# Weights of the output projections loaded piece by piece between the steps of other projections, each split one piece behind its DMA

## The chip, the cores and the metric

The kernel runs on one core of a Trainium2 chip. The metric is the device time of one execution in microseconds: the median of three runs, 1205.65 us before the change (1203.87 to 1205.76). The rows below come from one profiled execution of 1204.9 us, whose recorded span is 1203.1 us.

## The reference

A two-layer decoder trunk on x of 1024 tokens by 1024 columns, all in fp32 (P = 128 tokens make a block, so there are 8 blocks):

```
layer 0: h = rms_norm(x) * g;  z = h @ w_in
         z -> MLA q-latent, kv-latent, rope key | SWA q, k, v | gate
         MLA: 8 heads, causal attention          -> 512 columns
         SWA: 8 heads, window 128, ALiBi, sinks  -> 512 columns
         x1 = x + (concat(MLA, SWA) * silu(gate)) @ w_out      (1024x1024)
layer 1: h = rms_norm(x1) * g;  z = h @ w_in -> q, k, v, forget logits, gate
         16 heads, causal attention with cumulative log-forget bias
         x2 = x1 + (heads * silu(gate)) @ w_out                (1024x1024)
out = rms_norm(x2) * g_final
```

The change concerns the two products with `w_out`, the output projections.

## The kernel before, in words

Every fp32 product is made of three matmuls. An operand is split into a high part, the cast of the raw fp32 to fp32r, and a low part, raw minus high (`split_sb`, L109: the cast on ScalarE, L110, the subtraction on GpSimd or, if told so, VectorE, L111). `mm3` (L113) then adds high by high (L114), high by low and low by high (L115, L116). In the rows, `wh` and `wl` are the parts of an operand that lies in small tiles, `hh` and `hl` those of large ones: the normalised activations, and later the weights of the output projections. `kx` holds the weights of the windowed heads' output projection.

Every raw operand goes through the tag `wr`, which has four buffers (L74); `wh` and `wl` have three each. A DMA into `wr` can start when the split that reads that buffer's former content has ended. All these DMAs are issued by SyncE, in its own order.

Heads are the units of the main loop. A causal unit computes logits (`s`) row by row, the row's maximum (VectorE, L314), exponential (ScalarE, L321) and normalisation (GpSimd, L276), transposes the rows on PE (`t`, L347), splits them into `ph` (ScalarE, L102) and `pl` (VectorE, L103), and multiplies by v (`o`, L338 and L339). When a unit is done `o_evac` (L263) copies half of its output on ScalarE (`ob`, L267) and adds the rest on VectorE. Between these steps `Filler` runs steps of projections, one `mm3` at a time; strings of letters (`W_MLA_END` and so on) say where on PE each step stands, and PE's order is written by hand from them. The other engines' orders come from a scheduler that sees the program order and the buffers; an engine then takes its instructions in that fixed order.

`Filler` has two lists. `work` (projections) advances one step at a time; `loads` runs to its end at once as soon as its conditions are met. The output projections are these:

- `swa_wo(q)` (L888) loads four pieces of 128x512 of w_out's lower half for columns half q and splits each, in one go: for q = 0 as the load `wp`, for q = 1 in the last step of `p07` (L912). `swa_out(q, blk)` (L897), the work `p00` to `p07` and `p10` to `p17`, loads a 128x(4x128) operand of gated heads from `ogs0` (L901) and makes four steps.
- `load_wo` (L956) loads the other pieces: for layer 0 eight (four for each half of the columns) as the load `wo0` after `gate3`, the last gate projection; for layer 1 sixteen, eight of them when the first half of gate 6 is evacuated (`and_load`, L1140 on), the other eight two at a time in each `out1_first`. Its splits alternate between GpSimd and VectorE.
- `out0(nh, blk)` (L1018) and `out1_first(nh, blk)`, the work `first00` to `first13`, load their operand through `out_parts` (L971; DMA in L979) and make four steps each (`out_proj`, L986).

Of the kernel before, what the change touches and what calls it, by code (L numbers as in the profile page):

```python
# [18 lines left out]
P = 128  # L19
S = 1024  # L20
D = 1024
NB = S // P
# [37 lines left out]
def trunk(ctx, tc, x, positions, e_g_in, e_w_in, e_g_q_a, e_w_q_up, e_g_kv_a, e_w_kv_up,  # L60
# [45 lines left out]
            return nc.vector.scalar_tensor_tensor(out=lo, in0=src, scalar=gain, in1=hi.bitcast(F32),  # L106
                                                  op0=ALU.mult, op1=ALU.subtract).ins

    def split_sb(hi, lo, raw, engine=None):  # L109
        nc.scalar.copy(out=hi, in_=raw)  # L110
        (engine or nc.gpsimd).tensor_tensor(out=lo, in0=raw, in1=hi.bitcast(F32), op=ALU.subtract)  # L111

    def mm3(o, ah, al, bh, bl, first, last):  # L113
# [302 lines left out]
    class Filler:  # L416


        def __init__(self):
            self.work, self.loads, self.done = [], [], set()  # L420

        def add(self, name, gen, after=()):

# [2 lines left out]
        def load(self, name, gen, after=()):  # L426
            self.loads.append((name, gen, after))

        def free(self, items):
            return items and all(a in self.done for a in items[0][2])  # L430

        def ahead(self):

# [5 lines left out]

        def step(self):  # L440
            self.ahead()
            if self.free(self.work):
                try:
                    next(self.work[0][1])
                except StopIteration:
                    self.done.add(self.work.pop(0)[0])
                    self.step()

        def need(self, *names, ready=None):
            for name in names:  # L450
                while name not in self.done and not (ready and ready()):
                    self.ahead()
                    if name not in self.done:
                        assert self.free(self.work), (name, self.work[0], self.loads[:1])
                        self.step()

        def drain(self):
            while self.work or self.loads:
                self.ahead()
                assert self.free(self.work) or not self.work, self.work[0]  # L460
                self.step()

    fill = Filler()

# [421 lines left out]


    def swa_wo(q):  # L888
        tiles = [sbt("kx", [2, 512], F32R) for _ in range(4)]
        swa["wo"] = [(tiles[e // 2][:, e % 2, :], tiles[2 + e // 2][:, e % 2, :]) for e in range(4)]  # L890
        for e, (wh, wl) in enumerate(swa["wo"]):
            raw = sbt("wr", [512])
            for at, row in ((A, 512), (B, 768)):
                nc.sync.dma_start(out=raw[at], in_=wo0[row + 64 * e:row + 64 * e + 64, 512 * q:512 * (q + 1)])
            split_sb(wh, wl, raw)

    def swa_out(q, blk):  # L897
# [12 lines left out]
        nc.vector.tensor_tensor(out=r, in0=acc, in1=r, op=ALU.add)  # L910
        nc.sync.dma_start(out=xps[tok, cols], in_=r)
        if blk == NB - 1 and q == 0:  # L912
            swa_wo(1)
        yield

    def first_wo():
        swa_wo(0)
        yield

    units = []  # L920
    for _ in swa_q(0):
        pass
# [6 lines left out]
    for h in range(8):  # L929
        fill.load(f"prep{h}", mla_prep(h, heads[h]),  # L930
                  [[("rows", "swa", 5, 1)], [("rows", "swa", 7, 1), ("pv", "swa", 6, 1)],
                   [("rows", "mla", 0, 1), ("pv", "swa", 7, 1)]][h] if h < 3 else
                  [("rows", "mla", h - 2, 1), ("pv", "mla", h - 3, 1)])
        if h == 1:
            fill.load("wp", first_wo(), [("rows", "swa", 7, 1)])
    for pr in range(4):
        for d, G in UNIT_ORDER[pr == 3]:
            units.append(mla_unit(2 * pr + d, G))
    for w in WORK0.split():
        kind, i = w[0], int(w[1])  # L940
        if kind == "q":
            fill.add(f"qs{i}", swa_q(i), [("rows", "swa", 2 * i - 3, 1)] * (i > 1))
        elif kind == "s":
            fill.add(f"sgate{i}", gate_chunk(swa_gate(i), hT, None, ogs0[i]), [("pv", "swa", 2 * i + 1, 1)])
        elif kind == "p":
            q, blks = ((0, range(NB)), (1, range(4)), (1, range(4, NB)))[i]
            for blk in blks:
                fill.add(f"p{q}{blk}", swa_out(q, blk), ["wp", "sgate3", ("pv", "swa", 7, 1)])
# [7 lines left out]
    def load_wo(w, e0, halves):  # L956

        n = KC - e0
        for nh in range(2):
            if nh * n % KC == 0:  # L960
                th, tl = new_hT()
            a = nh * n % KC
# [2 lines left out]
            for e in range(n):  # L965
                raw = sbt("wr", [512])
                nc.sync.dma_start(out=raw, in_=w[e * P:(e + 1) * P, nh * 512:(nh + 1) * 512])
                split_sb(wh[:, e, :], wl[:, e, :], raw, nc.vector if e % 2 else nc.gpsimd)
                yield

    def out_parts(blk, ogs, own, e0s):  # L971

# [162 lines left out]

    FIRST = [0, 1, 2, 3]
    wo1_parts = []
    wo1_load = load_wo(wo1, 0, wo1_parts)

    def fox_gate(pr, halves=(0, 1)):  # L1140
        evac = gate_evac(fox[pr]["gt"])
# [6 lines left out]
        return project([(w1, FG + pr * P, FG + (pr + 1) * P)], hT, and_load, halves)  # L1148

    units = []  # L1150
    for pr in range(8):
# [27 lines left out]

    def out1_first(nh, blk):  # L1180
        parts = out_parts(blk, ogs1, None, [0])
        for _ in range(KC // len(FIRST)):
            next(wo1_load, None)
        yield from out_proj(nh, blk, parts, wo1_parts, x1s)
        yield

    def out1(blk):
# [18 lines left out]
        for nh in range(2):  # L1206
# [3 lines left out]
                nc.vector.tensor_scalar(out=y[nh], in0=y[nh], scalar1=r, scalar2=None, op0=ALU.mult)  # L1210
            nc.sync.dma_start(out=out[blk * P:(blk + 1) * P, nh * 512:(nh + 1) * 512], in_=y[nh])

    for nh in range(2):
        for blk in FIRST:
            fill.add(f"first{nh}{blk}", out1_first(nh, blk))
    for blk in range(NB):
        fill.add(f"out1{blk}", out1(blk), ["gfin", ("pv", "fox", 15, blk // 4)])
# [24 lines left out]
```

## Time and profile before

| | |
|---|---|
| median of 3 runs | 1205.65 us |
| profiled execution, its span | 1204.9 us, 1203.1 us |
| PE busy | 1161.3 us (97%) |
| VectorE busy | 738.1 us (61%) |
| ScalarE busy | 703.0 us (58%) |
| GpSimd busy | 587.8 us (49%) |
| granted clock, mean over the span | 0.993 |

PE is the engine that is nearly always busy, so a look at the time is a look at PE's gaps. In a timeline a row is an instruction (or a run of equal ones, "x4") with its start, its length, and in brackets the idle time of its engine just before it and the instruction whose end released it. "PE pj L116 MATMUL pj<-hh,wl" is the third matmul of a projection step; "<-POOL wl L111" says that it waited for GpSimd's subtraction.

### The profile page before, as it was taken

The page shows a single profiled execution, that of the slowest core. Times are in us where ns is not written, and L with a number is a line of the kernel's source. Part 1 is how long each engine was busy: PE and PEld are TensorE (multiplying, and loading weights), DVE is VectorE, ACT ScalarE, POOL GpSimd, SP SyncE. Part 2 cuts the span into 40 slices and gives each one's busy share as a digit, 9 for nine tenths or more (in the row PEclk, how much of TensorE's full clock was granted, in tenths as well). Part 3 has the DMA queues.
Part 4 walks back from the last instruction along what each step waited for, and adds up shares of the span by engine and source line. Part 5 has one row for each costly group of instructions (what it writes and reads, how often), then busy time and mean ns, then how long its engine had stood idle before and what let it go on. Part 6 is the DMA issues. An engine that isn't in the chain of part 4 may idle for free. (4 is left out here: it accounts for less than half of the span.)

```text
span 1203.1 us, 19942 instructions
## 1 busy us (share of the span) xinstructions
PE 1161.3 (97%) x6554; PEld 1001.6 (83%) x6554; DVE 738.1 (61%) x1946; ACT 703.0 (58%) x1583; POOL 587.8 (49%) x737
## 2 busy tenths in 40 slices
PE   4999999999989999999999999999999999999997
PEld 4997888888878877889998888888888888877886
DVE  8955466676775776665004666666656666657754
ACT  5634477776764765664214667666767676766532
POOL 5501154564654554434204555656555555567452
PEclk9999999999998999999999999999999999999999
DMA  6326522453653443574313222313131223247541
GB/s 213 85 51 221 164 45 62 130 152 123 167 162 94 123 142 98 171 217 119 99 49 103 63 79 62 89 53 88 55 96 61 82 69 101 66 128 223 172 162 61
DMA packets 157084, 135.27 MB, mean 112 GB/s; under 512 B 53259, under 2 KB 121638, under 8 KB 156982
## 3 DMA queue, kind: packets, MB, share of 16 engines
q1 hardware_dynamic: 156982, 134.02, 37.0%
q8 instruction: 51, 0.84, 0.3%
q14 instruction: 51, 0.42, 0.1%
HBM read 96.43 MB, written 37.55 MB: 111 GB/s over the span
## 5 line engine op out<-in xcount | busy, mean ns | idle before, releaser
L114 PE MATMUL pj<-hh,wh 128*128 128x512 f32 (+1 forms) x792 | 321.8, 406 | 1.6 <-ACT wh L110 1.6
L116 PE MATMUL pj<-hh,wl 128*128 128x512 f32 (+1 forms) x792 | 310.9, 393 | 6.0 <-POOL wl L111 6.0
L115 PE MATMUL pj<-hl,wh 128*128 128x512 f32 (+1 forms) x792 | 310.3, 392 | 0.0
L111 POOL TENSOR_TENSOR wl<-wr,wh 128x512 fp32r<-128x512 f32 (+1 forms) x130 | 162.7, 1253 | 164.3 <-ACT wh L110 153.0
L103 DVE TENSOR_TENSOR pl<-t,ph 128x512 fp32r<-128x512 f32 (+1 forms) x320 | 179.0, 564 | 83.8 <-ACT ph L102 81.6
L276 POOL TENSOR_SCALAR r<-r,sm 128x128 f32<-128x128 f32 (+4 forms) x248 | 167.1, 681 | 127.5 <-DVE sm L323 77.5
L102 ACT CAST ph<-t 128x512 fp32r<-128x512 f32 (+1 forms) x320 | 153.6, 483 | 111.9 <-PE t L347 93.1
L116 PEld LDWEIGHTS pj<-hh,wl 128*128 128x128 f32 x792 | 149.6, 189 | 39.6 <-POOL wl L111 7.3
L321 ACT ACTIVATE r<-r,sm 128x128 f32<-128x128 f32 (+7 forms) x184 | 143.1, 778 | 54.2 <-DVE sm L314 52.3
L114 PEld LDWEIGHTS pj<-hh,wh 128*128 128x128 f32 x792 | 150.1, 190 | 23.7 <-ACT wh L110 2.4
L115 PEld LDWEIGHTS pj<-hl,wh 128*128 128x128 f32 x792 | 150.5, 190 | 20.5
L347 PE MATMUL t<-ident,r 128*128 128x128 f32 x828 | 136.1, 274 | 5.7 <-DVE pl L103 3.6
L347 PEld LDWEIGHTS t<-ident,r 128*128 128x128 f32 x828 | 103.9, 141 | 33.8 <-DVE pl L103 5.0
L110 ACT CAST wh<-wr 128x512 fp32r<-128x512 f32 (+1 forms) x130 | 77.8, 598 | 59.9 <-PE pj L115 30.8
L308 POOL TENSOR_TENSOR ld<-ld,zrow 128x128 f32<-128x128 f32 x128 | 58.7, 468 | 99.9 <-DVE sm L314 77.8
L338 PE MATMUL o<-ph,v 128*128 128x512 f32 (+3 forms) x288 | 107.2, 372 | 0.0
L339 PE MATMUL o<-pl,v 128*128 128x512 f32 (+3 forms) x288 | 99.7, 347 | 0.0
L314 DVE CUSTOM_DVE_ANT_0 r<-s,ld 128x512 f32<-128x512 f32 (+1 forms) x120 | 67.6, 563 | 47.2 <-PE s L261 43.4
L285 POOL TENSOR_TENSOR v<-ge,v 128x512 fp32r<-128x512 f32 x26 | 34.5, 1328 | 72.4 <-ACT v L284 71.2
L338 PEld LDWEIGHTS o<-ph,v 128*128 128x128 f32 x288 | 54.6, 190 | 7.8
L339 PEld LDWEIGHTS o<-pl,v 128*128 128x128 f32 x288 | 54.8, 190 | 6.3
L114 PE MATMUL pj<-qh,hh 128*128 128x256 f32 (+1 forms) x176 | 51.0, 291 | 2.9 <-DVE r L649 2.1
(324 smaller groups left out, 2450.3 us busy)
## 6 DMA issues: line engine op xcount, KB each, us to landing
wr<-in_o_w_in SPq DMA_DIRECT2D x62, 256.0 KB, 3.3
ld<-lcs SPq DMA_DIRECT2D x16, 512.0 KB, 4.0
ogs<-og SPq DMA_DIRECT2D x28, 256.0 KB, 2.1
wr<-ogs SPq DMA_DIRECT2D x28, 256.0 KB, 3.9
ge<-vscr SPq DMA_DIRECT2D x24, 256.0 KB, 3.7
gt<-x1s SPq DMA_DIRECT2D x23, 256.0 KB, 2.9
wr<-ogs SPq DMA_DIRECT2D x24, 192.0 KB, 3.1
wr<-in_e_w_in SPq DMA_DIRECT2D x16, 256.0 KB, 3.1
```

The costliest lines, as they stand in the source:

```text
L102: nc.scalar.copy(out=hi, in_=src)
L103: nc.vector.tensor_tensor(out=lo, in0=src, in1=hi.bitcast(F32), op=ALU.subtract)
L110: nc.scalar.copy(out=hi, in_=raw)
L111: (engine or nc.gpsimd).tensor_tensor(out=lo, in0=raw, in1=hi.bitcast(F32), op=ALU.subtract)
L114: nc.tensor.matmul(out=o, lhsT=ah, rhs=bh, start=first, stop=False)
L115: nc.tensor.matmul(out=o, lhsT=ah, rhs=bl, start=False, stop=False)
L116: nc.tensor.matmul(out=o, lhsT=al, rhs=bh, start=False, stop=last)
L276: nc.gpsimd.tensor_scalar(out=row, in0=row, scalar1=rc, scalar2=scale, op0=ALU.mult, op1=ALU.mult)
L321: nc.scalar.activation(out=row[:, 0:L], in_=row[:, 0:L], func=AF.Exp, scale=-1.0, bias=mn, accum_out=den)
L338: nc.tensor.matmul(out=O[0][:, cols], lhsT=v()[:, j, :], rhs=ph[:, cols], start=j == 0, stop=False)
L339: nc.tensor.matmul(out=O[0][:, cols], lhsT=v()[:, j, :], rhs=pl[:, cols], start=False, stop=j == n - 1)
L347: nc.tensor.transpose(out=t[:, b * P:(b + 1) * P], in_=rows[b][:, j * P:(j + 1) * P], identity=ident)
```

## The change

`Filler` gets a third list, `sides`. A side is a generator with a number `every`: each second (or fourth) time that a projection step is taken, the first side whose conditions are met advances to its next yield. `unblock` advances it further when the next work waits for nothing but its pieces. The loads of w_out become sides: `wp0` and `wp1` (four pieces, one every four steps), `wo0` (eight, one every two steps, from the time when gate 3's first half is evacuated), `wo1a` and `wo1b` (eight each, one every two steps, the first from the evacuation of gate 6's first half, the second after the whole of gate 7). Each advance issues a piece's DMA and then the split of the piece before it; the cast in that split is kept at its place in the program's order (`keep_in_program_order`). Work that needs only the first four pieces waits for these alone. No arithmetic changes, and PE's instructions and their order are the same in both kernels.

```diff
-    def split_sb(hi, lo, raw, engine=None):
-        nc.scalar.copy(out=hi, in_=raw)
+    def split_sb(hi, lo, raw, engine=None, in_order=False):
+        cast = nc.scalar.copy(out=hi, in_=raw)
+        if in_order:
+            tc.keep_in_program_order(cast)
...
+        def advance(self):
+            if next(self.sides[0][1], self) is self:
+                self.done.add(self.sides.pop(0)[0])
+        def unblock(self):
+            while self.work and self.free(self.sides):
+                rest = self.missing(self.work)
+                if not rest or any((a[0] if type(a) is tuple else a) != self.sides[0][0] for a in rest):
+                    break
+                self.advance()
...
         def step(self):
             self.ahead()
+            self.unblock()
             if self.free(self.work):
+                if self.free(self.sides):
+                    self.ticks += 1
+                    if self.ticks % self.sides[0][3] == 0:
+                        self.advance()
...
     def swa_wo(q):
+        late = None
...
-            split_sb(wh, wl, raw)
+            if late:
+                late()
+            late = partial(split_sb, wh, wl, raw, None, True)
+            yield
+        late()
+        yield
...
-        if blk == NB - 1 and q == 0:
-            swa_wo(1)
...
+    fill.side("wp0", swa_wo(0), 4, [("rows", "swa", 7, 1)])
+    fill.side("wp1", swa_wo(1), 4, [f"p0{NB - 1}"])
...
-                split_sb(wh[:, e, :], wl[:, e, :], raw, nc.vector if e % 2 else nc.gpsimd)
+                if late:
+                    late()
+                    fill.done.add((name, pieces))
+                pieces += 1
+                late = partial(split_sb, wh[:, e, :], wl[:, e, :], raw, nc.vector if e % 2 else nc.gpsimd, True)
                 yield
+        late()
...
-    fill.load("wo0", load_wo(wo0, 4, wo), ["gate3", "sgate3"])
+    fill.side("wo0", load_wo("wo0", wo0, 4, wo), 2, [lambda: pairs[3]["gt"][0] is not None, "sgate3"])
-                fill.add(f"out0{nh}{blk}", out0(nh, blk), ["wo0", ("pv", "mla", 7, hf)])
+                fill.add(f"out0{nh}{blk}", out0(nh, blk), [("wo0", 4 * nh + 4), ("pv", "mla", 7, hf)])
...
-        def and_load(hf, acc):
-            evac(hf, acc)
-            if (pr, hf) == (6, 0):
-                for _ in range(KC):
-                    next(wo1_load)
...
-        for _ in range(KC // len(FIRST)):
-            next(wo1_load, None)
...
+    fill.side("wo1a", load_wo("wo1a", wo1, 0, wo1_parts, (0,)), 2, [lambda: fox[6]["gt"][0] is not None])
+    fill.side("wo1b", load_wo("wo1b", wo1, 0, wo1_parts, (1,)), 2, ["fgate7"])
-            fill.add(f"first{nh}{blk}", out1_first(nh, blk))
+            fill.add(f"first{nh}{blk}", out1_first(nh, blk), [("wo1" + "ab"[nh], 4)])
```

Line numbers in the rows of the changed kernel differ by a few from those before (L113 for L111, L278 for L276, L323 for L321, L269 for L267, L219 for L217).

GpSimd around the loading of the second half of the windowed heads' weights. The `kx` rows are the low parts of these weights, the last two `wl` rows (4552, 4558) the low parts of the weights of the projection that follows on PE, gate 1's second half; the rows with 512 to 1024 columns are normalisations of attention rows. Before:

```order
L276 TENSOR_SCALAR r_4261<-r_4261,sm_4268 128x512
L276 TENSOR_SCALAR r_4393<-r_4393,sm_4406 128x640
L111 TENSOR_TENSOR kx_4510<-wr_4512,kx_4508 128x512
L111 TENSOR_TENSOR kx_4510<-wr_4517,kx_4508 128x512
L285 TENSOR_TENSOR v_4588<-ge_4586,v_4588 128x8x64
L276 TENSOR_SCALAR r_4429<-r_4429,sm_4457 128x768
L276 TENSOR_SCALAR r_4467<-r_4467,sm_4480 128x896
L111 TENSOR_TENSOR kx_4511<-wr_4522,kx_4509 128x512
L111 TENSOR_TENSOR kx_4511<-wr_4527,kx_4509 128x512
L111 TENSOR_TENSOR wl_4552<-wr_4549,wh_4551 128x512
L111 TENSOR_TENSOR wl_4558<-wr_4555,wh_4557 128x512
L276 TENSOR_SCALAR r_4532<-r_4532,sm_4545 128x1024
```

After, where those two are `wl_4528` and `wl_4534`:

```order
L278 TENSOR_SCALAR r_4261<-r_4261,sm_4268 128x512
L113 TENSOR_TENSOR wl_4528<-wr_4525,wh_4527 128x512
L113 TENSOR_TENSOR wl_4534<-wr_4531,wh_4533 128x512
L278 TENSOR_SCALAR r_4393<-r_4393,sm_4406 128x640
L287 TENSOR_TENSOR v_4571<-ge_4569,v_4571 128x8x64
L278 TENSOR_SCALAR r_4429<-r_4429,sm_4457 128x768
L278 TENSOR_SCALAR r_4467<-r_4467,sm_4480 128x896
L113 TENSOR_TENSOR wl_4662<-wr_4659,wh_4661 128x512
L278 TENSOR_SCALAR r_4508<-r_4508,sm_4521 128x1024
L113 TENSOR_TENSOR wl_4668<-wr_4665,wh_4667 128x512
L278 TENSOR_SCALAR r_4577<-r_4577,sm_4584 128x128
L278 TENSOR_SCALAR r_4588<-r_4588,sm_4595 128x256
```

The two `wl` have moved from behind four `kx` and three normalisations to a place ahead of all of them; the `kx` have left this stretch for the places of later steps.

ScalarE around the end of gate 3 and the operands of `p14` and `p15`. Here `hh_5548` (before) and `hh_5443` (after) are pieces of `wo0`, `wh_5583` and `wh_5742` (before), `wh_5569` and `wh_5736` (after) the operands of `p14` and `p15`, `ob` the evacuation of a finished unit. Before:

```order
L110 CAST hh_5548<-wr_5578 128x512
L102 CAST ph_5476<-t_5471 128x512
L102 CAST ph_5495<-t_5491 128x384
L321 ACTIVATE r_5480,sm_5487<-r_5480,sm_5485 128x128
L110 CAST wh_5583<-wr_5582 128x512
L267 COPY ob_5503<-o_5396 64x512
L110 CAST wh_5742<-wr_5741 128x512
L102 CAST ph_5520<-t_5517 128x256
L110 CAST wh_5787<-wr_5786 128x512
```

After:

```order
L323 ACTIVATE r_5488,sm_5495<-r_5488,sm_5493 128x128
L102 CAST ph_5503<-t_5499 128x384
L269 COPY ob_5511<-o_5396 64x512
L110 CAST hh_5443<-wr_5472 128x512
L102 CAST ph_5532<-t_5529 128x256
L110 CAST hh_5443<-wr_5519 128x512
L219 ACTIVATE ge_5543<-pj_5429 128x512
L323 ACTIVATE r_5553,sm_5560<-r_5553,sm_5558 128x256
L110 CAST hh_5443<-wr_5536 128x512
L110 CAST wh_5569<-wr_5568 128x512
L110 CAST wh_5736<-wr_5735 128x512
L110 CAST hh_5443<-wr_5731 128x512
```

The casts of `p14` and `p15` have moved behind the `ob` copy, three casts of pieces, the gate's tanh and an exponential. What the order doesn't show is which buffers they wait for: the raw operand of `p14` (`wr_5568`) now goes into the buffer of the piece `wr_5472`, and that of `p15` (`wr_5735`) into the buffer of `wr_5568`.

ScalarE in layer 1, from the operand of `first01` to that of `first02`. `hh_13143` (before), `hh_12870` and `hh_13200` (after) are pieces of w_out. Before (the last row, `wh_13276`, is `first02`; `wh_13229`, `first01`, stands four rows ahead of the first):

```order
L267 COPY ob_13097<-o_12928 64x512
L102 CAST ph_13105<-t_13102 128x256
L217 ACTIVATE ge_13115<-pj_13013 128x512
L110 CAST hh_13143<-wr_13145 128x512
L110 CAST hh_13143<-wr_13149 128x512
L110 CAST hh_13143<-wr_13234 128x512
L102 CAST ph_13124<-t_13122 128x128
L110 CAST hh_13143<-wr_13238 128x512
L102 CAST ph_13164<-t_13159 128x512
L321 ACTIVATE r_13131,sm_13174<-r_13131,sm_13172 128x1024
L102 CAST ph_13187<-t_13183 128x384
L110 CAST wh_13276<-wr_13275 128x512
```

After, `wh_13227` is `first01` and `wh_13274` is `first02`:

```order
L110 CAST wh_13227<-wr_13226 128x512
L102 CAST ph_13177<-t_13173 128x384
L323 ACTIVATE r_13181,sm_13193<-r_13181,sm_13191 128x896
L269 COPY ob_13212<-o_13117 64x512
L102 CAST ph_13218<-t_13215 128x256
L110 CAST hh_13200<-wr_13202 128x512
L323 ACTIVATE r_13241,sm_13253<-r_13241,sm_13251 128x768
L110 CAST hh_13200<-wr_13222 128x512
L110 CAST hh_13200<-wr_13257 128x512
L110 CAST wh_13274<-wr_13273 128x512
```

`first01` has moved from a place between the exponentials of `kh` and `ql` to one behind the exponential of the 1024 row, and the first of the second eight pieces from ahead of that exponential to behind the one of the 896 row. Buffers: after, the raw operand of `first01` waits for the split of piece 7 (`wr_13103`), that of `first02` for the split of the piece `wr_13202`, whose cast is the sixth row, that of `first03` for the split of the piece `wr_13269`, which is cast two rows below `first02`, and that of `first10` for the split of `first03`'s own operand. That of `first00` waits for the split of piece 4 (`wr_12983`).

## Rows read from the trace of the kernel before

**Rows 1.** PE's timeline from 355 us: start, length, instruction, [idle before <-releaser]

```profile
356.81 0.50 PE L114 MATMUL pj<-hh,wh 128*128 128x512 f32 x1 [0.84 <-ACT wh L110]
...
362.53 0.79 PE L116 MATMUL pj<-hh,wl 128*128 128x512 f32 x1 [4.98 <-POOL wl L111]
```

**Rows 2.** Two windows: length, busy time (count) by engine, clock, DMA, GB/s

```profile
362.00:368.00 6.00, 5.47 (x14) 4.47 (x15) 0.00 (x0) 0.54 (x1) 4.04 (x4) 0.51 0.96 228
439.00:443.00 4.00, 4.00 (x16) 3.27 (x14) 1.81 (x4) 2.68 (x6) 1.99 (x2) 0.57 0.56 177
```

**Rows 3.** GpSimd's timeline, 350 to 366 us

```profile
356.78 3.48 POOL L111 TENSOR_TENSOR kx<-wr,kx 128x512 fp32r<-128x512 f32 x2
360.23 3.48 POOL L111 TENSOR_TENSOR wl<-wr,wh 128x512 fp32r<-128x512 f32 x2
```

**Rows 4.** PE's timeline, 437 to 465 us

```profile
438.04 0.79 PE L347 MATMUL t<-ident,r 128*128 128x128 f32 x3 [1.85 <-DVE pl L103]
...
447.47 0.40 PE L114 MATMUL pj<-kx,wh 128*128 128x512 f32 x1
...
463.69 0.33 PE L347 MATMUL t<-ident,r 128*128 128x128 f32 x1 [1.51 <-POOL r L276]
```

**Rows 5.** ScalarE's timeline, 443 to 447 us

```profile
444.76 0.61 ACT L110 CAST wh<-wr 128x512 fp32r<-128x512 f32 x1
445.39 0.58 ACT L267 COPY ob<-o 64x512 f32<-64x512 f32 x1
```

**Rows 6.** SyncE's timeline, 433 to 456 us

```profile
440.87 3.63 SPq L901 DMA_DIRECT2D wr<-ogs  x4
```

**Rows 7.** Last line of the view of L901, 300 to 500 us

```profile
DMA to landing us min/median/max: 2.8/3.5/5.0
```

**Rows 8.** PE's timeline, 1070 to 1104 us

```profile
1071.59 0.44 PE L347 MATMUL t<-ident,r 128*128 128x128 f32 x2 [1.47 <-DVE pl L103]
...
1074.44 0.50 PE L114 MATMUL pj<-hh,wh 128*128 128x512 f32 x1 [0.79 <-ACT wh L110]
...
1075.80 0.50 PE L116 MATMUL pj<-hh,wl 128*128 128x512 f32 x1 [0.62 <-POOL wl L111]
...
1085.06 0.39 PE L114 MATMUL pj<-hh,wh 128*128 128x512 f32 x1
...
1090.47 0.47 PE L114 MATMUL pj<-hh,wh 128*128 128x512 f32 x1
...
1094.03 0.39 PE L114 MATMUL pj<-hh,wh 128*128 128x512 f32 x1
...
1102.58 0.50 PE L116 MATMUL pj<-hh,wl 128*128 128x512 f32 x1 [0.36 <-POOL wl L111]
```

**Rows 9.** SyncE's timeline, 1066 to 1073 us

```profile
1069.51 0.94 SPq L151 DMA_DIRECT2D wr<-in_o_w_in  x2
1071.70 0.37 SPq L979 DMA_DIRECT2D wr<-ogs  x1
```

**Rows 10.** ScalarE's timeline, 1072 to 1074 us

```profile
1072.84 0.62 ACT L110 CAST hh<-wr 128x512 fp32r<-128x512 f32 x1 [1.64 <-DMA wr<-in_o_w_out]
1073.36 0.36 ACT L102 CAST ph<-t 128x256 fp32r<-128x256 f32 x1
```

**Rows 11.** VectorE's timeline, 1085 to 1087 us

```profile
1085.87 1.02 DVE L111 TENSOR_TENSOR hl<-wr,hh 128x512 fp32r<-128x512 f32 x1
```

**Rows 12.** Last line of the view of L979, 1060 to 1112 us

```profile
DMA to landing us min/median/max: 2.8/4.1/4.4
```

**Rows 13.** The page's costliest groups: count, busy us, mean ns | idle before

```profile
L111 POOL TENSOR_TENSOR wl<-wr,wh 128x512 fp32r<-128x512 f32 (+1 forms) x130 | 162.7, 1253 | 164.3 <-ACT wh L110 153.0
...
L102 ACT CAST ph<-t 128x512 fp32r<-128x512 f32 (+1 forms) x320 | 153.6, 483 | 111.9 <-PE t L347 93.1
...
L321 ACT ACTIVATE r<-r,sm 128x128 f32<-128x128 f32 (+7 forms) x184 | 143.1, 778 | 54.2 <-DVE sm L314 52.3
...
L110 ACT CAST wh<-wr 128x512 fp32r<-128x512 f32 (+1 forms) x130 | 77.8, 598 | 59.9 <-PE pj L115 30.8
```

More of the change, by code (lines that the diff above doesn't have):

```diff
@@ L420, in __init__ @@
             self.work, self.loads, self.done = [], [], set()
+            self.sides, self.ticks = [], 0
         def add(self, name, gen, after=()):
@@ L427, in load, with side, missing @@
             self.loads.append((name, gen, after))
+        def side(self, name, gen, every, after=()):
+            self.sides.append((name, gen, after, every))
+        def missing(self, items):
+            return [a for a in items[0][2] if not (a() if callable(a) else a in self.done)]
         def free(self, items):
-            return items and all(a in self.done for a in items[0][2])
+            return items and not self.missing(items)
+        def advance(self):
[7 more added lines that the diff above has]
+                self.advance()
         def ahead(self):
@@ L453, in need @@
                     if name not in self.done:
+                        self.unblock()
                         assert self.free(self.work), (name, self.work[0], self.loads[:1])
@@ L459, in drain @@
                 self.ahead()
+                self.unblock()
                 assert self.free(self.work) or not self.work, self.work[0]
                 self.step()
+            while self.sides:
+                self.advance()
     fill = Filler()
@@ L911, in swa_out @@
         nc.sync.dma_start(out=xps[tok, cols], in_=r)
-        if blk == NB - 1 and q == 0:
-            swa_wo(1)
         yield
-    def first_wo():
-        swa_wo(0)
-        yield
+    fill.side("wp0", swa_wo(0), 4, [("rows", "swa", 7, 1)])
+    fill.side("wp1", swa_wo(1), 4, [f"p0{NB - 1}"])
     units = []
@@ L933, in trunk @@
                   [("rows", "mla", h - 2, 1), ("pv", "mla", h - 3, 1)])
-        if h == 1:
-            fill.load("wp", first_wo(), [("rows", "swa", 7, 1)])
     for pr in range(4):
@@ L947, in trunk @@
             for blk in blks:
-                fill.add(f"p{q}{blk}", swa_out(q, blk), ["wp", "sgate3", ("pv", "swa", 7, 1)])
+                fill.add(f"p{q}{blk}", swa_out(q, blk), [f"wp{q}", "sgate3", ("pv", "swa", 7, 1)])
         else:
@@ L953, in trunk, with load_wo @@
                      [("pv", "mla", 2 * i - 3, 1)] * (i > 1))
-    def load_wo(w, e0, halves):
-        n = KC - e0
-        for nh in range(2):
+    def load_wo(name, w, e0, halves, nhs=(0, 1)):
+        n, pieces, late = KC - e0, 0, None
+        for nh in nhs:
             if nh * n % KC == 0:
@@ L967, in load_wo @@
                 nc.sync.dma_start(out=raw, in_=w[e * P:(e + 1) * P, nh * 512:(nh + 1) * 512])
-                split_sb(wh[:, e, :], wl[:, e, :], raw, nc.vector if e % 2 else nc.gpsimd)
+                if late:
[3 more added lines that the diff above has]
+                late = partial(split_sb, wh[:, e, :], wl[:, e, :], raw, nc.vector if e % 2 else nc.gpsimd, True)
                 yield
+        late()
+        fill.done.add((name, pieces))
+        yield
     def out_parts(blk, ogs, own, e0s):
@@ L1137, in trunk @@
     wo1_parts = []
-    wo1_load = load_wo(wo1, 0, wo1_parts)
     def fox_gate(pr, halves=(0, 1)):
-        evac = gate_evac(fox[pr]["gt"])
-        def and_load(hf, acc):
-            evac(hf, acc)
-            if (pr, hf) == (6, 0):
-                for _ in range(KC):
-                    next(wo1_load)
-        return project([(w1, FG + pr * P, FG + (pr + 1) * P)], hT, and_load, halves)
+        return project([(w1, FG + pr * P, FG + (pr + 1) * P)], hT, gate_evac(fox[pr]["gt"]), halves)
     units = []
@@ L1211, in out1 @@
             nc.sync.dma_start(out=out[blk * P:(blk + 1) * P, nh * 512:(nh + 1) * 512], in_=y[nh])
+    fill.side("wo1a", load_wo("wo1a", wo1, 0, wo1_parts, (0,)), 2, [lambda: fox[6]["gt"][0] is not None])
+    fill.side("wo1b", load_wo("wo1b", wo1, 0, wo1_parts, (1,)), 2, ["fgate7"])
     for nh in range(2):
         for blk in FIRST:
-            fill.add(f"first{nh}{blk}", out1_first(nh, blk))
+            fill.add(f"first{nh}{blk}", out1_first(nh, blk), [("wo1" + "ab"[nh], 4)])
     for blk in range(NB):
-        fill.add(f"out1{blk}", out1(blk), ["gfin", ("pv", "fox", 15, blk // 4)])
+        fill.add(f"out1{blk}", out1(blk), ["gfin", "wo1a", "wo1b", ("pv", "fox", 15, blk // 4)])
     with tc.manual_schedule(engines={mybir.EngineType.PE}):
```

## The prediction

> **What bounds the kernel now.** I read the page first: PE is busy nearly all the time, so the change can only act through PE's gaps. I then went through PE's timeline for the gaps that lie where the four loads of w_out are, looked up in the other engines' timelines what each gap waited for, and last took the new order of ScalarE, GpSimd and SyncE beside it, buffer by buffer.
>
> There are three places. *The second windowed-head load*, before `p10`: PE waits 0.84 us for a cast and 4.98 us for a low part of gate 1's weights [rows 1]. GpSimd is late with it because it first makes two low parts of `kx`, 3.48 us, and then two of gate 1, 3.48 us [rows 3]. The wait costs more than its length: in the six microseconds after it the granted clock is 0.51 in the mean, the lower of PE's two levels, 1.2 of 2.4 GHz, nearly all the time [rows 2]. *Layer 0's own load*: PE waits 1.85 us for `pl` at 438.04 [rows 4], held up by eight splits in a row, and from 439 to 443 the mean clock is 0.57 [rows 2]. *Layer 1's load*: waits of 1.47, 0.79 and 0.62 us between 1070 and 1076 [rows 8]. The first windowed-head load (`wp0`, near 205 us) has no such gap, and I cost its move at nothing: its pieces end tens of microseconds ahead of `p00`.
>
> **The change part by part.** No instruction is added or removed and PE's order is the same, so the sum holds waits alone. Durations: a cast on ScalarE 0.60 us, an exponential 0.78 in the mean, a `ph` 0.48, a split on GpSimd 1.25 [rows 13], one on VectorE 1.0 [rows 11]. From a DMA's issue to its landing 2.8 us at least, 3.5 or 4.1 in the median [rows 7, 12]; I take 2.8, because the transfers in the chains below go out one at a time, where the medians hold batches such as the four raw operands in 3.63 us [rows 6]. The Trainium skill has another value: in "DMA: Bandwidth & Descriptors", section "Anatomy of one DMA — SWDGE (gpsimd) path", one transfer costs about 2.0 us plus its bytes at 436 GB/s, an estimate of 2.6 us for these 256 KB. The rows show none below 2.8; with 2.6 the eight landings of the two chains below would be 1.6 us shorter together and the sum 1.6 lower.
>
> *Gate 1, near 360 us.* Its two `wl` stand ahead of all `kx` now, behind the 512 row. Both waits go, 5.8 us. The half clock goes too: 5.47 us of PE's work at 0.51 [rows 2] would take 2.7 less at full clock. Together 8.5. What is late next I put at 0.8: PE arrives 8.5 us earlier at logits whose operands VectorE splits, and the cast of `p10`'s operand stands in front of `ph` casts. The bounds are 0 and 1.85 (a cast and a split of rows 13). Term: -7.7, from -8.5 to -6.65.
>
> *`p14` to `p17`, near 447 us.* The wait of 1.85 goes, and of 4.0 us at a mean clock of 0.57 [rows 2] 1.7: a gain of 3.5. But see what the operands of `p14` to `p17` do. Before, SyncE issued all four in one run from 440.87 [rows 6], and `p14` was cast at 444.76, ahead of `ob` [rows 5], 2.7 us before PE wanted it at 447.47 [rows 4]. Now `p14`'s raw operand waits for the buffer of piece 1, whose cast stands behind `ob`. In the times of before: `ob` 444.8 to 445.4 (0.6 earlier than its row, the cast in front of it being gone), the piece's cast to 446.0, its split on VectorE to 447.05, the transfer to 449.85, `p14`'s cast to 450.45, its split to 451.7. PE's third matmul of `p14` was due at 447.94: 3.8 late. Then `p15`'s operand waits for the buffer of `p14`: landed 454.5, cast 455.1. PE needs it only near 460, but ScalarE takes its instructions in order, and behind this cast stand the exponentials of the 384 and 512 rows. A row of before shows that such a cast holds what is behind it: after 1.64 us of waiting for a DMA, `hh` at 1072.84, and only then at 1073.36 the `ph` [rows 10] whose transposes, at 1071.59 [rows 8], were long done. Two casts, a `ph` and two exponentials after 455.1 end at 458.4; `p16`'s cast, after its own transfer, at 460.35; then four `ph`, four exponentials and three casts or copies, 6.9 us, to 467.3, and with the normalisation the transposes that started at 463.69 [rows 4] come at about 468.5. The long rows take more than the mean exponential, so I say 469.7, 6.0 late. Against the gain of 3.5 this is a loss: +2.5. From -3.5 (nothing late) to +4.6 (three landings of 3.5).
>
> *Layer 1, 1070 to 1103 us.* Before, gate 7's weights were issued from 1069.51 and `first00`'s operand at 1071.70 [rows 9], 13 us before PE used it at 1085.06 [rows 8]. Of the 2.9 us of waits about 1.0 is gained: the weights are issued no earlier than before, behind piece 1's split, and PE comes 1.5 us earlier. From here each `first` waits for a buffer that is freed by a split standing, on ScalarE, behind the cast of the `first` before. `first00` waits for piece 4, cast behind the exponential of a 256 row, at about 80.5, and split at 82.4 (times less 1000). Landed 85.2, cast 85.8, split 87.1. PE's third matmul of it, at 85.5 before: +1.6. `first01` waits for piece 7, cast behind `first00`, the gate's tanh and a `ph`: cast 87.3, split 88.3, landed 91.1, cast 91.7, split 93.0, against 91.0: +2.0. `first02` waits for the piece cast after `first01`, a `ph`, an exponential, an `ob` and a `ph`: 94.9; split 96.1, landed 98.9, cast 99.5, split 100.8, against 94.5: +6.3. `first03` waits for a piece cast behind `first02` and behind a `ph` whose transposes come after `first02`'s first steps on PE: 102.7; split 103.7, landed 106.5, cast 107.1, split 108.3. `first10` waits for `first03`'s split: landed 111.1, cast 111.7, split 113.0, against 1102.58 [rows 8], the row that already held a wait of 0.36: +10.4.
> After it the operands come in ahead of PE and the delay stays. Bounds: -2.9 (no chain) and +16.9 (five landings of 4.1).
>
> Sum: -7.7 + 2.5 + 10.4 = +5.2 on the profiled execution's 1204.9 gives 1210.1. That run lies between the median, 1205.65, and the lowest of the three, so I add 0.4 and predict 1210.5.
>
> **The rivals.**
> *The gains alone.* The orders put the casts late, but each transfer has slack enough. For it: before the change the same four buffers served `first00` to `first03` with waits of only 0.36 us [rows 8]. Against: they were issued 13 us ahead then. -8.5 - 3.5 - 2.9 = -14.9: 1190.
> *Half the chains.* Splits run sooner than I place them, so that layer 1 loses about 4 and `p14` breaks even with its gain: -7.7 + 0 + 4 = -3.7, about 1202 by the same base.
> *The clock falls again.* `p14` and `first02` stop PE for about 4 us each, as long as the gap that ended at 362.53 [rows 1] and was followed by half clock [rows 2]. The half clock cost 2.7 there. Where the next wait in a chain is for a transfer it is hidden; it counts after the last link, once or twice: 1213 to 1216. The Trainium skill says the same against this change in "TensorE: Matmul & The Clock Gate", section "Why this matters for your kernels": a gap between bursts of matmuls sends the array back to its slow rate. The trace agrees at both gaps, 4.98 and 1.85 us.
> *The change does not act.* The waits near 360 are taken over by the next late cast and the chains don't bind: about 1205.
>
> **How the numbers follow.** Chances: the forecast 0.50, the clock rival 0.12, half the chains 0.18, the gains alone 0.13, no effect 0.07. About 0.2%, 2.4 us, is what a measurement here can tell from no change: 1203.2 to 1208.1 is the same. Slower: the forecast and the clock, with a little of the rest, 0.64. Faster: the gains alone and half of the half-chains, 0.22. The same: 0.14. The likeliest case's own range is 1206 to 1219. For eight in ten I leave out the gains alone and the end where all landings are medians: 1198 to 1219.
>
> **What would show it.** Near 360 GpSimd's `wl` of gate 1 ahead of `kx`, no wait of PE above 1 us and a clock of 1.00. A wait of PE of about 4 us at the third matmul of `p14`, with SyncE issuing `p14` to `p17` one by one. In layer 1 waits on `wh` and `wl` at every `first`, the longest, about 4 us, at `first02`, and 20 us or more from `first00` to `first03`. The prediction is wrong if the operands of `p14` and `first02` are issued some 3 us ahead of these times, that is, if the casts that free their buffers don't wait where the order has them.

## The result, and the profile after

The change makes the kernel slower: 1219.28 us in the median of four runs (1216.80 to 1220.62) against 1204.76 (1203.85 to 1205.76), a ratio of 1.0118 with an interval of 1.0098 to 1.0138, or 14.5 us. The forecast was 1210.5 us with 1198 to 1219: the right direction and about a third of the size. The profiled execution took 1220.6 us, its span 1218.8, which is 15.7 more than before, at a mean clock of 0.986.

PE's timeline first (start and length in us, instruction, idle time before it and what released it). `mm3` starts at L115 now, so that its three lines are L116 to L118, and a low part is made in L113.

```profile
354.02 0.48 PE L116 MATMUL pj<-kx,wh 128*128 128x512 f32 x1
...
357.29 0.39 PE L118 MATMUL pj<-hh,wl 128*128 128x512 f32 x1
...
428.56 0.49 PE L349 MATMUL t<-ident,r 128*128 128x128 f32 x3
...
439.04 0.80 PE L116 MATMUL pj<-kx,wh 128*128 128x512 f32 x1 [2.79 <-ACT wh L110]
...
440.39 0.79 PE L118 MATMUL pj<-kx,wl 128*128 128x512 f32 x1
...
461.06 0.33 PE L349 MATMUL t<-ident,r 128*128 128x128 f32 x1 [0.77 <-POOL r L278]
...
1068.10 0.38 PE L349 MATMUL t<-ident,r 128*128 128x128 f32 x2
...
1084.88 0.51 PE L116 MATMUL pj<-hh,wh 128*128 128x512 f32 x1 [0.95 <-ACT wh L110]
...
1092.90 0.48 PE L116 MATMUL pj<-hh,wh 128*128 128x512 f32 x1
...
1102.32 0.79 PE L116 MATMUL pj<-hh,wh 128*128 128x512 f32 x1 [5.71 <-ACT wh L110]
...
1103.68 0.80 PE L118 MATMUL pj<-hh,wl 128*128 128x512 f32 x1
...
1110.74 0.50 PE L116 MATMUL pj<-hh,wh 128*128 128x512 f32 x1 [1.35 <-ACT wh L110]
...
1117.18 0.56 PE L118 MATMUL pj<-hh,wl 128*128 128x512 f32 x1 [0.63 <-POOL wl L113]
```

PE's order is the same in both kernels, so the start of an instruction after, less its start before, is the balance up to there. It starts with something that isn't the change's: PE is 1.06 us behind when it comes to gate 1's place, 354.02 against

```profile
352.96 0.48 PE L114 MATMUL pj<-kx,wh 128*128 128x512 f32 x1
```

before. It fell behind near 34 us, ahead of the first piece, where the clock of this execution is 0.51 and that of before 1.00 (first row of the windows below). Near 360 the wait of 4.98 us [rows 1] is gone: the matmul that stood behind it starts at 357.29, and some six microseconds on, with the half clock gone too, PE is 7.8 us ahead, and 7.5 from 380 on. Layer 0's own load gives its 1.85 us and its half clock [rows 4, 2]: 428.56 is 9.5 us ahead of 438.04, and the balance reaches -11.4. Then come the operands of `p14` to `p17`: 440.39, the third matmul of `p14`, stood at 447.94 before (-7.55), and 461.06 answers to 463.69 (-2.6). Some 0.8 us more are lost by 1055 us, most of them near 540, where one wait for VectorE is 1.22 us long and was 0.61. In layer 1 two waits for gate 7's weights (1.54 and 0.62 us near 1072, where before had 1.47, 0.79 and 0.62) and the waits of `first00`, `first02`, `first03` and `first10` turn -3.5 (1068.10 against 1071.59 [rows 8]) into +14.6 (1117.18 against 1102.58). At half clock behind the last of them it becomes +15.7, and stays there to the end.

Windows of after: the stretch and its length, the busy time (count) of PE, its weight loads, VectorE, ScalarE and GpSimd, then the mean clock, the DMA share and GB/s:

```profile
32.00:35.50 3.50, 3.50 (x19) 3.50 (x18) 3.43 (x8) 2.74 (x11) 3.15 (x6) 0.51 0.42 113
357.00:363.00 6.00, 6.00 (x32) 5.18 (x32) 5.22 (x14) 4.77 (x9) 3.37 (x4) 1.00 0.57 192
439.00:445.00 6.00, 5.83 (x14) 4.54 (x15) 0.56 (x2) 1.31 (x4) 1.89 (x2) 0.50 0.60 192
1066.00:1124.00 58.00, 44.63 (x187) 34.19 (x186) 26.75 (x66) 28.38 (x60) 32.90 (x32) 0.85 0.53 167
...
1073.00:1077.50 4.50, 4.49 (x16) 3.77 (x17) 1.43 (x5) 1.65 (x4) 2.54 (x4) 0.62 0.43 150
...
1110.70:1115.80 5.10, 3.30 (x12) 2.10 (x12) 2.71 (x4) 3.07 (x6) 4.19 (x3) 1.00 0.59 186
1117.50:1121.00 3.50, 3.50 (x12) 2.77 (x11) 0.00 (x0) 0.62 (x1) 2.14 (x2) 0.51 0.76 234
```

The first stretch in before:

```profile
32.00:35.50 3.50, 3.50 (x32) 3.50 (x31) 3.43 (x8) 2.77 (x11) 3.13 (x6) 1.00 0.41 114
```

Near 360 the clock is full, where it was 0.51 [rows 2]. Behind `p14`'s wait it is at the lower level, and 0.85 in the mean over layer 1's chain. (The last three windows are for the last section.)

Why `p14` and `first02` are late is read on the queues. SyncE of after (issues by their start and length):

```profile
435.41 0.38 SPq L939 DMA_DIRECT2D wr<-ogs  x1
...
440.36 0.38 SPq L939 DMA_DIRECT2D wr<-ogs  x1
...
1093.75 0.33 SPq L1039 DMA_DIRECT2D x1s<-gt  x1
1097.89 0.33 SPq L1030 DMA_DIRECT2D gt<-x1s  x1
1098.31 0.39 SPq L1018 DMA_DIRECT2D wr<-ogs  x1
```

Waits of SyncE, 1060 to 1125 us (in total, times, longest):

```profile
SPq L1030 <- DMA x1s<-gt: 7.1, 3, 3.8
```

ScalarE of after:

```profile
438.37 0.62 ACT L110 CAST wh<-wr 128x512 fp32r<-128x512 f32 x1 [0.40 <-DMA wr<-ogs]
...
443.69 0.62 ACT L110 CAST wh<-wr 128x512 fp32r<-128x512 f32 x1 [4.70 <-DMA wr<-ogs]
...
1091.00 0.62 ACT L110 CAST wh<-wr 128x512 fp32r<-128x512 f32 x1 [0.57 <-DMA wr<-ogs]
...
1093.15 1.05 ACT L323 ACTIVATE r<-r,sm 128x896 f32<-128x896 f32 x1 [1.16 <-DVE sm L316]
...
1095.19 0.62 ACT L110 CAST hh<-wr 128x512 fp32r<-128x512 f32 x1
...
1101.65 0.62 ACT L110 CAST wh<-wr 128x512 fp32r<-128x512 f32 x1 [2.35 <-DMA wr<-ogs]
```

GpSimd of after:

```profile
444.38 1.29 POOL L113 TENSOR_TENSOR wl<-wr,wh 128x512 fp32r<-128x512 f32 x1 [4.05 <-ACT wh L110]
445.63 1.30 POOL L113 TENSOR_TENSOR hl<-wr,hh 128x512 fp32r<-128x512 f32 x1
...
1095.90 1.28 POOL L113 TENSOR_TENSOR hl<-wr,hh 128x512 fp32r<-128x512 f32 x1 [0.29 <-ACT hh L110]
```

Where four operands of `p14` to `p17` were issued in one run of 3.63 us [rows 6], `p14`'s and `p15`'s are now 5 us apart. ScalarE casts `p14`'s operand when it lands, and then stands 4.70 us until `p15`'s lands, with everything that is queued behind that cast. In layer 1 one link of the chain can be followed from row to row: `first01` is cast at 1091.00; behind it ScalarE waits 1.16 us for the maximum of a logits row; the piece is cast at 1095.19 and split until 1097.18; `first02`'s operand is issued at 1098.31 into that buffer, behind a load of `gt` for which SyncE has waited until the store of `x1s`, issued at 1093.75, has landed; it is cast at 1101.65, and PE goes on at 1102.32.

### The profile page after: what moved, and what is told of

Same layout as the page of the kernel before. It is cut to its first block, busy times and chain, and to the rows that moved or that the text cites. A ratio compares the mean times of both kernels' runs of the same rounds, so it can differ in the third digit from the quotient of the medians.

```text
span 1218.8 us, 19931 instructions
## 1 busy us (share of the span) xinstructions
PE 1169.2 (96%) x6554; PEld 1005.9 (83%) x6554; DVE 732.7 (60%) x1946; ACT 704.3 (58%) x1583; POOL 586.1 (48%) x737
## 5 line engine op out<-in xcount | busy, mean ns | idle before, releaser
L116 PE MATMUL pj<-hh,wh 128*128 128x512 f32 (+1 forms) x792 | 322.1, 407 | 11.1 <-ACT wh L110 10.7
L118 PE MATMUL pj<-hh,wl 128*128 128x512 f32 (+1 forms) x792 | 310.8, 392 | 2.7 <-POOL wl L113 2.5
L113 POOL TENSOR_TENSOR wl<-wr,wh 128x512 fp32r<-128x512 f32 (+1 forms) x130 | 162.1, 1248 | 173.8 <-ACT wh L110 164.4
L278 POOL TENSOR_SCALAR r<-r,sm 128x128 f32<-128x128 f32 (+4 forms) x248 | 168.3, 687 | 120.1 <-DVE sm L325 74.4
L118 PEld LDWEIGHTS pj<-hh,wl 128*128 128x128 f32 x792 | 149.6, 189 | 37.6 <-POOL wl L113 5.1
L116 PEld LDWEIGHTS pj<-hh,wh 128*128 128x128 f32 x792 | 149.8, 189 | 34.3 <-ACT wh L110 12.6
L323 ACT ACTIVATE r<-r,sm 128x128 f32<-128x128 f32 (+7 forms) x184 | 143.0, 777 | 53.5 <-DVE sm L316 51.5
L116 PE MATMUL pj<-qh,hh 128*128 128x256 f32 (+1 forms) x176 | 51.4, 293 | 3.3 <-DVE r L681 1.9
```

The lines of the kernel that those rows point to most:

```text
L116: nc.tensor.matmul(out=o, lhsT=ah, rhs=bh, start=first, stop=False)
L118: nc.tensor.matmul(out=o, lhsT=al, rhs=bh, start=False, stop=last)
L278: nc.gpsimd.tensor_scalar(out=row, in0=row, scalar1=rc, scalar2=scale, op0=ALU.mult, op1=ALU.mult)
L323: nc.scalar.activation(out=row[:, 0:L], in_=row[:, 0:L], func=AF.Exp, scale=-1.0, bias=mn, accum_out=den)
```

## The experiments

The times stand against the runs of the kernel before that were made beside them (1205.4 to 1206.3 in the median), the intervals are those of the ratio. "After" in the comparisons is the changed kernel.

**One load at a time.** The three loads of the change, each made a side alone, the others loaded as before (`load_wo_old` is the `load_wo` of before). The first, with the windowed heads' load alone:

```diff
-    fill.side("wo0", load_wo("wo0", wo0, 4, wo), 2, [lambda: pairs[3]["gt"][0] is not None, "sgate3"])
+    fill.load("wo0", load_wo_old(wo0, 4, wo), ["gate3", "sgate3"])
...
-    fill.side("wo1a", load_wo("wo1a", wo1, 0, wo1_parts, (0,)), 2, [lambda: fox[6]["gt"][0] is not None])
-    fill.side("wo1b", load_wo("wo1b", wo1, 0, wo1_parts, (1,)), 2, ["fgate7"])
```

> Only the two loads of the windowed heads' weights are sides; layer 0's and layer 1's own loads are made as before. If the trace of the changed kernel can be read part by part (PE 7.8 us ahead of before between 368 and 438 us), this keeps that gain alone: 1204.8 - 7.8 = 1197, and PE's waits near 438 and 1071 are those of before. If the lead is lost again at the next places for reasons of its own (another wait takes over), it lies above 1200.

Measured: 1197.79, ratio 0.9935 (0.9915 to 0.9955), 8.5 us faster.

The second, with layer 0's own load alone (`wp0`, `wp1`, `wo1a` and `wo1b` as before):

> Only layer 0's own eight pieces are a side, the rest as before. By the trace of the changed kernel PE gains 3.5 us near 438 and loses 8.4 between 447 and 464, and another 0.9 near 542: 1204.8 + 5 to 6 = 1210. If the loss there came from the windowed heads' pieces before it (their buffers, or PE arriving 8 us earlier than the transfers), it is about 1202.

Measured: 1209.36, ratio 1.0028 (1.0014 to 1.0041), 3.4 us slower.

The third, with layer 1's load alone:

> Only layer 1's sixteen pieces are sides, the rest as before. By the trace of the changed kernel PE loses 17.2 us between 1055 and 1110 of before: 1204.8 + 17 = 1222, with the longest wait, over 5 us, at first02. If part of that loss is only the lead of 1.8 us given back, it is 1220; if it needs the other parts of the change, it is below 1215.

Measured: 1222.05, ratio 1.0134 (1.0118 to 1.0149), 16.1 us slower. PE's timeline of this run has the wait of `first02`:

```profile
1105.56 0.80 PE L116 MATMUL pj<-hh,wh 128*128 128x512 f32 x1 [6.25 <-ACT wh L110]
```

The three add up to +11.0, the whole change is +14.5; each of the four has an interval of about 2 us to either side, so the 3.5 between can be noise or an interaction. One term is a clear gain, one a small loss, and layer 1's load alone costs more than the whole.

**What the chain is made of.** Three things make it up: raw buffers that pieces and operands share, casts that are held at their place in the program, and a split that comes one piece behind its DMA. One is taken away at a time. Buffers of their own for the pieces (small tiles `sm` cut from 32 to 24 to make room):

```diff
-            "wr": (4, 2048), "wh": (3, 2048), "wl": (3, 2048),
+            "wr": (4, 2048), "wq": (2, 2048), "wh": (3, 2048), "wl": (3, 2048),
...
-            raw = sbt("wr", [512])
+            raw = sbt("wq", [512])
```

> All as in the changed kernel, but the pieces have two raw buffers of their own instead of sharing the four of the operands (the 32 small statistics buffers become 24 to make room). If the loss comes from the shared buffers, an operand waiting for the late split of a piece, the waits at p14 and at first00 to first10 go and with them the half clock behind them: 1190 to 1196. If the loss comes from the casts that stand at their place in the program order and hold ScalarE, whatever buffers they use, most of it stays: 1212 or more.

Measured: 1195.00, ratio 0.9915 (0.9893 to 0.9937). No cast of an operand is among PE's waits from 425 to 1125 us (total, times, longest):

```profile
PE t L349 <- POOL r L278: 4.7, 4, 2.0
PE t L349 <- DVE pl L103: 2.9, 1, 2.9
```

At the place of `first10` PE is 15.5 us ahead of before, and loses 6 of them in the next few microseconds (the waits of 2.9 and 2.0 us, and half clock): exponentials stand behind casts of pieces that wait for their DMA. In after the same view, of the whole span, has

```profile
PE pj L116 <- ACT wh L110: 13.5, 6, 5.7
...
PE pj L118 <- POOL wl L113: 2.5, 4, 0.7
```

Casts free to be scheduled:

```diff
-        if in_order:
-            tc.keep_in_program_order(cast)
```

> All as in the changed kernel, but without keep_in_program_order on the pieces' casts: the scheduler may move them up, the split still comes one piece behind in the program. If the fixed place of the cast is what holds the buffers, p14 is cast ahead of ob again and the chain goes: 1190 to 1198. If the four shared buffers and the split one piece behind are enough for it, it stays at 1215 to 1220.

Measured: 1198.84, ratio 0.9945 (0.9927 to 0.9963), again with no wait for an operand's cast.

The split right behind its DMA, buffers and pinned casts as in after (`load_wo` is changed in the same way):

```diff
-            if late:
-                late()
-            late = partial(split_sb, wh, wl, raw, None, True)
+            split_sb(wh, wl, raw, None, True)
```

> All as in the changed kernel, but each piece's split follows its own DMA in the program instead of coming one piece later; the cast keeps its place and the four buffers stay shared. If the loss is the time for which a piece holds a shared buffer, it shrinks: the buffer is free two steps (about 2 us) earlier at each link, the eight links give back some 8 to 12 us, 1207 to 1211. If a cast that stands in ScalarE's order right behind its own transfer now waits there for the landing, some 3 us for each piece, and holds the exponentials behind it, it grows: 1222 or more.

Measured: 1211.21, ratio 1.0043 (1.0028 to 1.0058): 8 to 9 of the 14.5 us come back. PE's waits of this run:

```profile
PE pj L118 <- POOL wl L113: 7.2, 5, 3.3
PE pj L116 <- ACT wh L110: 3.4, 1, 3.4
```

The operands are still late, but by less. The two chains cost PE 26 us on the trace of after (8.8 near `p14`, 17.5 in layer 1) and 17 in this run (5.2 and 12.0): the late split makes about a third of what the chain costs. Net of the gains that is more than half of the 14.5 us.

Six shared buffers instead of four and two apart (`sm` at 24 here too):

```diff
-            "wr": (4, 2048), "wh": (3, 2048), "wl": (3, 2048),
+            "wr": (6, 2048), "wh": (3, 2048), "wl": (3, 2048),
```

> The changed kernel with six raw buffers, shared by pieces and operands, where it had four. If what counts is how many transfers back the split lies that an operand waits for, two more buffers put it two transfers back, some 4 to 6 us at each link, and nearly all goes: 1193 to 1198, like four and two apart. If it counts that operands and pieces are apart, because an operand then waits only for operands, most of the loss stays: 1206 or more.

Measured: 1204.57, ratio 0.9987 (0.9978 to 0.9996), between the two expectations. The chain is shorter, not gone; PE's timeline of this run near `first03`:

```profile
1094.53 0.50 PE L116 MATMUL pj<-hh,wh 128*128 128x512 f32 x1 [2.66 <-ACT wh L110]
1095.88 0.80 PE L118 MATMUL pj<-hh,wl 128*128 128x512 f32 x1 [0.62 <-POOL wl L113]
```

Four and two apart take some 9 us less than six shared, but only part of that is the chain. In its profiled execution the kernel with six shared buffers is 3.8 us behind before already at the start, ahead of the first piece (the order of SyncE's loads is another one there). Before and this run:

```profile
53.58 0.28 PE L115 MATMUL pj<-ql,hh 128*128 128x256 f32 x1
```

```profile
57.39 0.32 PE L117 MATMUL pj<-ql,hh 128*128 128x256 f32 x1
```

Of the 26 us of the two chains 7 are left with six shared (2.3 and 4.8) and 4 with buffers apart (1.9 and 2.3), on one trace of each. Two more buffers take most of the chain away by their number; keeping pieces and operands apart adds some 3 us. (The smaller `sm` was not run alone.)

**The clock.** PE is given dummy matmuls, whose results are overwritten, while it waits: 11 ahead of `p14`, 4, 22, 6 and 5 ahead of `first00`, `first02`, `first03` and `first10`.

```diff
+    def busy(acc, w, n):
+        for _ in range(n):
+            nc.tensor.matmul(out=acc, lhsT=w[:, 0:P], rhs=w, start=True, stop=True)
```

> The changed kernel with matmuls added on PE whose results are overwritten by the product that follows: 11 ahead of p14, 4 ahead of first00, 22 ahead of first02, 6 ahead of first03, 5 ahead of first10, each lot some 0.2 to 0.7 us shorter than the wait that PE has there. If the half clock behind these waits costs time of its own, as PE's distance to before grows by 2.9 us behind p14 and by some 6 us behind the others, the time falls by 6 to 9 us, to 1210 to 1213. If the next wait of the chain hides it, as the prediction held, the time stays within 2 us of 1219.

Measured: 1218.43, ratio 1.0105 (1.0085 to 1.0124), the time of after. Two windows of this run, columns as above:

```profile
436.00:445.00 9.00, 8.17 (x37) 6.29 (x37) 3.58 (x11) 3.71 (x10) 3.52 (x4) 1.00 0.65 204
1066.00:1124.00 58.00, 50.15 (x235) 38.82 (x235) 29.87 (x69) 30.50 (x64) 34.68 (x34) 0.97 0.56 168
```

The clock is 1.00 and 0.97 in place of 0.50 and 0.85 (it falls to 0.50 later here, from 448.7 to 452.0), and the operands come 0.4 us earlier. PE's timeline, beside 1102.32 and 1103.68 of after:

```profile
1101.88 0.50 PE L116 MATMUL pj<-hh,wh 128*128 128x512 f32 x1 [0.64 <-ACT wh L110]
...
1103.23 0.50 PE L118 MATMUL pj<-hh,wl 128*128 128x512 f32 x1 [0.62 <-POOL wl L113]
```

On the trace layer 1 loses 15.2 us in place of 17.5 and `p14` to `p17` 5.2 in place of 4.9; the 0.9 between the medians is within the intervals. PE at half clock so costs some 2 us here and not 6 to 9, since it waits for the next link of the chain anyway. (The dummy matmuls don't cover the wait near 1071.)

**What is left without the chain.** Own buffers, with layer 1's load as before:

> The windowed heads' and layer 0's pieces as sides with two raw buffers of their own, layer 1's loads as before. The kernel with own buffers throughout was 11.5 us ahead of before at 1055 and lost 5 us again near 1105, behind its last pieces. If that loss is layer 1's alone, this keeps the 11.5: 1193 to 1194, 1 to 2 us better than own buffers throughout.

Measured: 1193.89 (1191.34 to 1194.53), ratio 0.9892 (0.9874 to 0.9909), 12.0 us faster than before: the lowest of all, though the 1.1 us to own buffers throughout are within the scatter.

Own buffers without the pinned casts:

> Own buffers for the pieces throughout and the casts free to move. Own buffers alone lost 5 us near 1105 while ScalarE stood behind casts of pieces that waited for their transfers. If the fixed place makes these waits, the free casts give 3 to 5 us back: 1190 to 1192. If the scheduler, as without the pin and with shared buffers (1199), puts casts ahead of exponentials, it is 1195 to 1199.

Measured: 1205.53, ratio 0.9994 (0.9984 to 1.0003). I had expected a gain on either theory; both are wrong. PE waits for softmax in this run:

```profile
PE s L114 <- DVE sm L314: 4.1, 4, 2.0
...
PE s L260 <- DVE sm L314: 3.2, 3, 2.0
...
PE t L347 <- POOL qh L276: 2.6, 1, 2.6
```

So the pinned cast, a part of the chain while the buffers are shared, is worth some 10 us once they are apart: 1195.0 with it, 1205.5 without. Which casts the scheduler then puts ahead of which exponentials I did not follow one by one.

The best version without the pinned casts:

> Own buffers and sides for the windowed heads' and layer 0's pieces, layer 1 as before, casts free to move. With the casts in place this took 1193.9. If the fixed place is of use once the buffers are apart, it is slower, 1196 or more; if it makes no difference there, within 2 us of 1194.

Measured: 1198.85, ratio 0.9942 (0.9928 to 0.9957), 5 us slower than with them.

Own buffers with the second half of layer 1's pieces at every fourth step, to take their casts out of the exponentials' way:

```diff
-    fill.side("wo1b", load_wo("wo1b", wo1, 0, wo1_parts, (1,)), 2, ["fgate7"])
+    fill.side("wo1b", load_wo("wo1b", wo1, 0, wo1_parts, (1,)), 4, ["fgate7"])
```

> Own buffers throughout, casts in place, and layer 1's second eight pieces one every four steps instead of two. With two, ScalarE waited for the transfers of five pieces in front of the exponential of the 640 row, and PE lost 5 us behind it; now two pieces stand in front of it. If that is what cost the 5 us, PE keeps its lead of 15 us over before: 1189 to 1191. If the pieces now come too late for first10 to first13, PE waits there instead and it is 1194 or more.

Measured: 1195.52, ratio 0.9918 (0.9901 to 0.9934). The wait of the exponentials is gone, and the pieces come too late for `first10` instead, as PE's timeline shows:

```profile
1092.14 0.50 PE L116 MATMUL pj<-hh,wh 128*128 128x512 f32 x1 [1.69 <-ACT hh L110]
...
1093.50 0.50 PE L117 MATMUL pj<-hl,wh 128*128 128x512 f32 x1 [0.86 <-POOL hl L113]
```

## Why the prediction was right in sign and too small

**Gate 1, -7.7.** The balance reads -7.8, but it starts at +1.06 (354.02), which was lost near 34 us at half clock. The place itself gives 8.9, 5.8 of them the two waits, and 0.3 is given back by 380: -8.5 for the term, and -8.5 us for this load alone. Wait and half clock are confirmed; most of the 0.8 kept back is not, and that -7.8 lies next to -7.7 is luck.

**`p14` to `p17`, +2.5.** The gain is there, 3.9 against 3.5: -7.5 becomes -11.4. (What held `pl` up before was not eight splits in a row, but VectorE's two, 3.04 us long, behind four casts.) `p14`'s third matmul was put 3.8 late and is 3.8 late (-11.4 to -7.55); its operand was to be issued at 435.7 on after's scale (447.05 less the lead of 11.4) and is issued at 435.41. The end is 8.8 late (-11.4 to -2.6) instead of 6.0. The term comes out at +4.9 on the trace (-7.5 to -2.6), above the +4.6 that I had as the end for slow landings; layer 0's load alone, with a smaller lead, cost +3.4. The landings are part of it: 2.96, 3.33 and 3.0 us from issue to cast for `p14` to `p16`, 0.9 more than three times 2.8. Another 0.8 is GpSimd, which starts the split of the piece that `p16` waits for at 445.63, behind `p15`'s own, where I had it start when its cast ended (444.82).

**Layer 1, +10.4.** This is the step that failed, by its size: +17.5 on the trace (-1.8 before it, +15.7 at the end), above the +16.9 of its range, and +16.1 for this load alone. Of the 7.1 us missed 3.0 are the one link shown above. From the cast of `first01` to the third matmul of `first02` I had 9.7 us and it took 12.7: 1.0 more until the piece's cast had ended, because ScalarE waits for VectorE's maximum, where I had queued its instructions back to back; 0.2 more to the end of the split; 1.1 between the end of the split and the issue, where I had none, because SyncE sends a load of `gt` first, which itself waits for a store to land; 0.5 for a landing of 3.34 instead of 2.8; 0.1 behind it. The rest is 1.7 ahead of this link, 1.3 in the links behind it and 1.1 after the last, where the clock of 0.51 has no wait behind it that would hide it. (The 1.0 that I had as gained at gate 7's weights is not gained either, but `first00` waits behind it.) The landing was mis-sized all along the chain. From issue to cast the five operands took 3.1, 3.5, 3.34, 2.8 and 3.06 us, 15.8 where the sum has 14.0. The views of L1018 (1060 to 1122 us) and of L939 (425 to 460 us) end in

```profile
DMA to landing us min/median/max: 3.0/3.2/4.2
```

```profile
DMA to landing us min/median/max: 2.9/3.0/3.3
```

The medians of before, 3.5 and 4.1 [rows 7, 12], were too long for this chain, as I argued, but the shortest landing was not its price either. Durations of work were right: casts, splits and exponentials cost what they did in [rows 13].

**Sum.** +5.2 predicted, +15.7 on the trace: 7.1 from layer 1, 2.4 from `p14` to `p17`, 0.8 between the two, which I had not seen, 1.1 from the first 36 us, which is not the change's, and -0.8 from gate 1 (rounded). What was wrong is that each link of the chains was priced at its least, with no other wait of the engines and queues in it, so that the errors had one sign. The top of my range took in longer landings and no waits of that kind.

**The rivals.** "The gains alone" fails, and so does "the change does not act": the chains bind, and the experiments that take them away give 1194 to 1199, not quite 1190. "Half the chains" lies below, not above. "The clock falls again" is right in that it falls (0.50 near 440) and wrong as a cost of some microseconds: with the clock kept up the time is the same within the intervals. I had said that it is hidden where the next wait is for a transfer and counts after the last link, and that is what the trace shows, with 1.1 us there. The Trainium skill's rule in "TensorE: Matmul & The Clock Gate", section "Why this matters for your kernels", that gaps drop the array to its slow rate, holds here for the clock behind the long waits (2.79 and 5.71 us), and hardly for the time.

**The marks.** They came as announced near 360 and at `first02`, where PE waits 5.71 us instead of about 4; `first01` did not wait, and `p14` waits at its first matmul (2.79 us, for the cast) rather than at its third. Not tried apart: ScalarE's wait for the maximum, SyncE's order and the landing; their shares are read from the trace alone.

## What to carry to other kernels

A prefetch that shares a small ring of buffers with the operands it runs beside can turn parallel transfers into a chain of DMA, cast and split; give it more buffers, best of its own, before spreading it, and only then choose the order of its casts. When a chain's links are added up from rows, each link needs the waits of the in-order engines and of the issuing queue as well, and the landing as it is among other traffic: least values in every link err on one side. Half clock behind a gap cost little here where PE's next wait was late anyway, and it cost in full behind the last wait.

## What the hardware showed that I had not expected

The clock does not follow the length of a gap alone. Before, waits of 1.47, 0.79 and 0.62 us within five microseconds [rows 8] left PE at full clock (1.00 from 1070 to 1080). In after a wait of 1.54 us and one of 0.62, at 1071.66 and 1073.01, are followed by a mean of 0.62 from 1073.0 to 1077.5; 1.35 and 0.63 us, at 1110.74 and 1112.10, by 1.00; and 1.15 and 0.63, at 1115.82 and 1117.18, by 0.51. What makes the difference the runs don't tell.
